# A decoder layer on one core: the feed-forward's input forms made in two steps, row inverses by a product

## The chip, the core and the metric

The kernel runs on one core of a Trainium2 chip. Its engines work in parallel and wait for each other by semaphores: TensorE (PE, matmuls; PEld is its weight load), VectorE (DVE), ScalarE (ACT), GpSimd (POOL), and SyncE (SP, which issues most DMAs). The metric is the device time of one execution, in microseconds.

## What is computed

The layer normalises x, mixes tokens by two kinds of attention, projects the merged mixers and adds the result to the residual. A SwiGLU feed-forward and a last normalisation follow. The part that matters here is the second half:

```python
x = x + merged @ w_out[i]
u2 = rms_norm(x, norm_ffn_g[i])
g_ff, up_ff = jnp.split(u2 @ w_ffn_in[i], 2, axis=-1)
x = x + (jax.nn.silu(g_ff) * up_ff) @ w_ffn_out[i]
return rms_norm(x, norm_final_g)
```

There are 512 tokens, the model is 1024 wide (8 blocks of 128 features) and the feed-forward 2816 wide (22 blocks).

## The kernel before

Everything is kept transposed: features on the 128 partitions, tokens along the free axis. `xall` holds the residual, 8 blocks of 128x512. Each fp32 operand of a matmul is split into a high part (rounded by a copy on ACT) and a low part (the difference, on DVE), and each product is three matmuls: high by high, high by low, low by high (L734, L735, L736, or L157 to L159). Weights come in chunks of 128x1024, split in the same way (L142 on ACT, L143 on DVE); "weights 62" is chunk 62, whose parts the order calls whi62 and wlo62. Three chunks of split weights are held.

**Output projection** (L693 to L702). A loop over f in the order 0, 4, 1, 5, 2, 6, 3, 7 multiplies the merged mixers by one chunk of w_out (24 matmuls of 512 columns), adds the residual into `xall[f]` on DVE (L699), squares it on ACT (L181) and adds the square into `acc2` on POOL (L183). Two PSUM banks alternate. After f = j + 4, `forms(j)` makes what the feed-forward reads of blocks j and j + 4.

**Forms.** The product with w_ffn_in is done by a scheme of 2x2 blocks that needs seven products instead of eight. For it the blocks x[j] and x[j+4], scaled by their gains and cut into two halves of 256 tokens, give B11 and B12 (from x[j]), B21 and B22 (from x[j+4]), and the sums T3 = B22 - B12, U1 = B11 - B12, V2 and T4. The high parts are `fh[j]`, the low parts `fl[j]`, seven pieces of 256 columns each. `forms` runs four multiplies on ACT (L683), splits B11 and B21, makes the four sums on DVE (L685 to L688), and splits the other five pieces together.

**Hidden blocks** (L722). `hidden(i)` runs seven products of 12 matmuls of 256 columns (four j, three matmuls each) in two PSUM banks, `pf` and `pg`. Copies of half-finished sums are kept by ACT (`kept`: q1, q7, wv, yv). It uses four chunks: 62 to 65 for i = 0, 66 to 69 for i = 1, 70 to 73 for i = 2. Because the scale by row comes after the products, block 0 also runs the row statistics: `row_sums` (ss, four sums by matmul from acc2, and r = ms to the power -0.5 on POOL) and `row_spread` (a diagonal matrix dg, one fp32 matmul rb that spreads the row factors over the partitions, and a copy).

**Scaling of the residual.** The feed-forward's rows are not multiplied by the last row factor, so the residual is divided by it instead: after block 1, `scale_residual` takes the reciprocal of the spread row factors on DVE (L715) and multiplies `xall` by it, two blocks at a time (L717). From block 6 on, `down` (the second feed-forward matrix, L808) adds partial products into `xall`.

**Order.** TensorE's instructions follow the order of the code in the feed-forward (`manual_schedule`, L847). On the other engines a scheduler sets the order ahead of time, with `high_priority` for what stands in such a block; on the chip each engine works through its list in order.

Of the kernel before, what the change touches and what calls it, by code (L numbers as in the profile page):

```python
# [10 lines left out]
F32 = mybir.dt.float32  # L11
# [3 lines left out]
ALU = mybir.AluOpType  # L15

P = 128
S = 512
D = 1024
KD = D // P  # L20
# [23 lines left out]
def trunk_kernel(ctx, tc, xT, gains, w_in, w_up, w_o, w_f, w_d, bias, out):  # L44
# [6 lines left out]
    V, A, G, T = nc.vector, nc.scalar, nc.gpsimd, nc.tensor  # L51
# [41 lines left out]
    for step in FFN:  # L93
        if step[0] == "in":
            i = step[1]
            chunks += [("A1", w_f[2 * i], 1024), ("S23", w_f[2 * i + 1], 1024), ("S1", None, 1024), ("S4", None, 512)]
        else:
            _, p, f = step
# [62 lines left out]
    def split_to(hi, lo, src):  # L161
        A.copy(hi, src)  # L162
        V.tensor_tensor(out=lo, in0=src, in1=hi.bitcast(F32), op=ALU.subtract)  # L163
# [15 lines left out]
    def norm_square(k, x, acc, name):  # L179
        sq = acc if k == 0 else sqp.tile([P, S], F32, tag="sq", name=f"sq{name}_{k}")  # L180
        A.activation(sq, x, AF.Square)  # L181
        if k:
            G.tensor_tensor(out=acc, in0=acc, in1=sq, op=ALU.add)  # L183
# [73 lines left out]
    def row_factors(acc, sq, n, name, ps=None, eps=None):  # L257
        if ps is None:
            ps = bank("att", f"ss{name}")
        for t in (acc, sq):  # L260
            for j in range(n if t is not None else 0):
                T.matmul(ps[:, j:j + 1], blk(t, j // 4, j % 4), ones[:, 0:1], start=t is acc and j == 0,
                         stop=t is sq or sq is None, skip_group_check=True)
        ms = cp.tile([P, 8], F32, tag="ms", name=f"ms{name}")
        if eps is None:
            V.tensor_scalar(out=ms[:, :n], in0=ps[:, :n], scalar1=1.0 / D, scalar2=EPS, op0=ALU.mult, op1=ALU.add)
        else:
            V.scalar_tensor_tensor(out=ms[:, :n], in0=ps[:, :n], scalar=1.0 / D, in1=eps, op0=ALU.mult, op1=ALU.add)
        if name == "2":
            rows["eps"] = cp.tile([P, 4], F32, tag="eps", name="eps")  # L270
            V.tensor_scalar_mul(rows["eps"], ms[:, :4], EPS)
        r = cp.tile([P, 8], F32, tag="r", name=f"r{name}")
        G.tensor_tensor(out=r[:, :n], in0=ms[:, :n], in1=mh[:, :n], op=ALU.pow)
        return r
# [63 lines left out]
    def next_weights(ahead=2):  # L338
        w = weights(ci[0], ahead)
        ci[0] += 1  # L340
        return w
# [330 lines left out]
    acc2 = cp.tile([P, S], F32, tag="acc", name="acc2")  # L672
    xall = fp.tile([P, KD, S], F32)
    fh, fl = [], []
    B11, B21, T3, V2, U1, T4, B22 = range(7)

    def forms(j):
        raw = fp.tile([P, 7, hs], F32, tag="form", name=f"form{j}")
        b12 = fp.tile([P, hs], F32, tag="b12", name=f"b12{j}")
        hi = fp.tile([P, 7, hs], F32R, tag=f"fh{j}", name=f"fh{j}")  # L680
        lo = fp.tile([P, 7, hs], F32R, tag=f"fl{j}", name=f"fl{j}")
        for o, k, c in ((raw[:, B11, :], j, 0), (raw[:, B21, :], j + 4, 0), (raw[:, B22, :], j + 4, hs), (b12, j, hs)):
            A.mul(o, xall[:, k, c:c + hs], gt[:, 8 + k:9 + k])  # L683
        split_to(hi[:, 0:2, :], lo[:, 0:2, :], raw[:, 0:2, :])
        V.tensor_tensor(out=raw[:, T3, :], in0=raw[:, B22, :], in1=b12, op=ALU.subtract)  # L685
        V.tensor_tensor(out=raw[:, U1, :], in0=raw[:, B11, :], in1=b12, op=ALU.subtract)
        V.scalar_tensor_tensor(out=raw[:, V2, :], in0=raw[:, B22, :], scalar=-1.0, in1=raw[:, U1, :], op0=ALU.mult, op1=ALU.subtract)
        V.scalar_tensor_tensor(out=raw[:, T4, :], in0=raw[:, V2, :], scalar=-1.0, in1=raw[:, B21, :], op0=ALU.mult, op1=ALU.subtract)  # L688
        split_to(hi[:, 2:, :], lo[:, 2:, :], raw[:, 2:, :])
        fh.append(hi)  # L690
        fl.append(lo)

    for f in HALVES:  # L693
        x = xall[:, f, :]
        nc.gpsimd.dma_start(out=x, in_=xT[f])
        ps = bank("proj", f"po{f}")
        product(ps, mhi, mlo, next_weights(), KD)
        with tc.high_priority():
            V.tensor_tensor(out=x, in0=ps, in1=x, op=ALU.add)  # L699
        norm_square(f, x, acc2, "2")  # L700
        if f >= 4:
            forms(f - 4)  # L702

    def row_sums():
        rows["r2"] = row_factors(acc2, None, 4, "2")
# [4 lines left out]

    def scale_residual():
        inv = sqp.tile([P, S], F32, tag="sq", name="inv")
        V.reciprocal(inv, rows["rb2"])  # L715
        for f in range(0, KD, 2):
            V.tensor_tensor(out=xall[:, f:f + 2, :], in0=xall[:, f:f + 2, :], in1=inv.unsqueeze(1).to_broadcast([P, 2, S]), op=ALU.mult)  # L717


    hh, hl = {}, {}  # L720
# [1 line left out]
    def hidden(i):  # L722
# [15 lines left out]
        def kept(ps, name):  # L738
            t = fp.tile([P, hs], F32, tag=f"kept{name}", name=f"{name}{i}")
            with tc.high_priority():  # L740
                A.copy(t, ps)  # L741
            return t

        w[0] = next_weights()
        if i == 0:

            w[1] = next_weights()
            times(pa, 0, 0, B11, range(3), first=True)
            times(psum, 0, 1, B21, range(3), first=True)
            times(pr, 1, 1, T3, range(3))  # L750
            times(pa, 0, 0, B11, [3])
            q1 = kept(pa, "q1")
            times(psum, 0, 1, B21, [3], last=True)
            times(pr, 1, 1, T3, [3])
            q7 = kept(pr, "q7")
            times(pa, 1, 0, V2)
            wv = kept(pa, "wv")
            with tc.high_priority():
                row_sums()
        else:  # L760
            times(pa, 0, 0, B11, first=True)
            q1 = kept(pa, "q1")
            times(psum, 0, 1, B21, first=True, last=True)
            w[1] = next_weights()
            times(pa, 1, 0, V2)
            wv = kept(pa, "wv")
            times(pr, 1, 1, T3)
            q7 = kept(pr, "q7")
        w[2] = next_weights()
        if i == 0:  # L770
            times(pr, 2, 1, T4, last=True)
# [36 lines left out]
    def down(f, p, w, cs=slice(0, S)):  # L808
        ps = bank("proj", f"pd{p}{f}")[:, cs]
        ks = PARTS[p]  # L810
        product(ps, [hh[k][:, cs] for k in ks], [hl[k][:, cs] for k in ks], w, len(ks))
        x = xall[:, f, cs]
        V.tensor_tensor(out=x, in0=ps, in1=x, op=ALU.add)
        if p < 3:
            return
        if f < KD - 1:
            sq = acc3 if f == 0 else sqp.tile([P, S], F32, tag="sq", name=f"sq3_{f}")
            A.activation(sq[:, cs], x, AF.Square)
            if f:
                G.tensor_tensor(out=acc3[:, cs], in0=acc3[:, cs], in1=sq[:, cs], op=ALU.add)  # L820
        else:
            A.activation(lsq[:, cs], x, AF.Square)
        A.mul(x, x, gt[:, 16 + f:17 + f])
# [25 lines left out]
    for step in FFN:  # L849
        if step[0] == "in":  # L850
            hidden(step[1])
            if step[1] == 1:
                scale_residual()
        elif step[1] < 3 or step[2] < 4:
            down(step[2], step[1], next_weights())
    ws = [next_weights(3 - j) for j in range(4)]
# [92 lines left out]
```

## Time and profile before

| | us |
|---|---|
| median of 3 runs | 782.24 |
| the three runs | 778.64, 782.24, 783.12 |
| the profiled execution | 779.83 |
| its span, first to last instruction | 778.1 |
| TensorE busy | 757.5 |
| DVE busy | 515.6 |
| ACT busy | 363.3 |
| POOL busy | 41.8 |

Matmuls overlap, so the distance from one start to the next tells what one costs, not its own duration. A row of the timeline gives the start, the duration, the engine, the line, the operation and its tiles; in brackets stands how long the engine was idle before it and who released it.

### The profile page before, as it was taken

What the parts mean: (1) busy time and instruction counts of PE and PEld (TensorE: products, weight loads), DVE (VectorE), ACT (ScalarE), POOL (GpSimd) and SP (SyncE); (2) the same over time, 40 slices, a digit from 0 to 9 for tenths busy, and PEclk for the clock granted to TensorE, in tenths of its full rate; (3) what the DMA queues carried; (4) which work ended last, traced back from release to release, by engine and by line L of the source; (5) the groups of instructions that cost most, each with busy time, mean ns of one, the idle gap of its engine ahead of it and who ended that gap; (6) DMA issues with size and microseconds to landing.
All of it is one profiled execution on the core that took longest, in us unless ns stands there. A gap on an engine that the chain in (4) does not pass through costs nothing.

```text
span 778.1 us, 10997 instructions
## 1 busy us (share of the span) xinstructions
PE 757.5 (97%) x4469; PEld 647.7 (83%) x4469; DVE 515.6 (66%) x674; ACT 363.3 (47%) x520; POOL 41.8 (5%) x46
## 2 busy tenths in 40 slices
PE   8999999999999999999997899999999999999994
PEld 5876767788877878888786899999999999999983
DVE  6343636434777773376886999886778777776543
ACT  7273736643223532332664556554445454444362
POOL 1000000000100100002321000000000000000032
PEclk9999999999999999999997999999999999999998
DMA  7421212023222223234521232333333333332113
GB/s 243 136 76 61 81 55 82 28 82 116 74 82 82 73 91 95 64 112 171 183 80 55 81 103 92 111 96 102 96 102 115 103 88 106 113 102 75 43 53 109
DMA packets 24947, 74.13 MB, mean 95 GB/s; under 512 B 2736, under 2 KB 5824, under 8 KB 24768
## 3 DMA queue, kind: packets, MB, share of 16 engines
q1 hardware_dynamic: 23536, 69.74, 28.0%
q0 software_dynamic: 816, 3.16, 1.1%
q8 instruction: 35, 0.57, 0.3%
q10 hardware_dynamic: 544, 0.52, 0.2%
q14 instruction: 16, 0.13, 0.1%
HBM read 71.32 MB, written 2.10 MB: 94 GB/s over the span
## 4 chain that ended last, share of the span: by engine, by line
PE 87%; DVE 7%; ACT 2%; DMA 1%; issue 1%; SPq 0%; POOL 0%; DVEq 0%; ACTq 0%; POOLq 0%
PE pd L157 5%; PE pd L158 5%; PE pd L159 5%; PE pf L736 5%; PE pf L735 5%; PE pf L734 5%; PE pg L734 4%; PE pg L735 4%; PE pg L736 4%; PE pjgs L157 2%; PE pjgd L157 2%; PE pjgs L159 2%; PE pjgd L159 2%; PE pjgs L158 2%; PE pjgd L158 2%; PE pvvd L157 2%
## 5 line engine op out<-in xcount | busy, mean ns | idle before, releaser
L142 ACT CAST whi<-raw 128x1024 fp32r<-128x1024 f32 (+2 forms) x113 | 108.5, 962 | 155.0 <-issue 49.2
L143 DVE TENSOR_TENSOR wlo<-raw,whi 128x1024 fp32r<-128x1024 f32 (+2 forms) x113 | 126.1, 1117 | 36.6 <-ACT whi L142 36.0
L736 PE MATMUL pf<-fh,wlo 128*128 128x256 f32 x352 | 100.4, 285 | 2.1 <-DVE wlo L143 2.1
L734 PE MATMUL pf<-fh,whi 128*128 128x256 f32 x352 | 100.6, 286 | 1.6 <-ACT fh L162 1.0
L735 PE MATMUL pf<-fl,whi 128*128 128x256 f32 x352 | 100.3, 285 | 1.1 <-DVE fl L163 1.1
L734 PE MATMUL pg<-fh,whi 128*128 128x256 f32 x264 | 76.1, 288 | 0.8 <-ACT fh L162 0.8
L735 PE MATMUL pg<-fl,whi 128*128 128x256 f32 x264 | 75.5, 286 | 0.9 <-DVE fl L163 0.9
L736 PE MATMUL pg<-fh,wlo 128*128 128x256 f32 x264 | 75.3, 285 | 0.0
L734 PEld LDWEIGHTS pf<-fh,whi 128*128 128x128 f32 x352 | 68.2, 194 | 3.6 <-ACT yv L741 1.6
L736 PEld LDWEIGHTS pf<-fh,wlo 128*128 128x128 f32 x352 | 68.1, 194 | 2.7 <-DVE wlo L143 2.7
L735 PEld LDWEIGHTS pf<-fl,whi 128*128 128x128 f32 x352 | 68.1, 194 | 1.9 <-DVE fl L163 1.3
L157 PE MATMUL pd<-hh,whi 128*128 128x512 f32 (+1 forms) x184 | 69.3, 377 | 0.0
L158 PE MATMUL pd<-hl,whi 128*128 128x512 f32 (+1 forms) x184 | 69.2, 376 | 0.0
L159 PE MATMUL pd<-hh,wlo 128*128 128x512 f32 (+1 forms) x184 | 69.0, 375 | 0.0
L143 DVE TENSOR_TENSOR wlo<-s,whi 128x1024 fp32r<-128x1024 f32 (+1 forms) x44 | 42.1, 957 | 17.9 <-ACT whi L142 17.9
L734 PEld LDWEIGHTS pg<-fh,whi 128*128 128x128 f32 x264 | 51.3, 194 | 1.5 <-ACT fh L162 1.0
L735 PEld LDWEIGHTS pg<-fl,whi 128*128 128x128 f32 x264 | 51.3, 194 | 1.2 <-DVE fl L163 1.2
L142 ACT CAST whi<-s 128x1024 fp32r<-128x1024 f32 (+1 forms) x44 | 36.8, 837 | 31.1 <-PE pg L735 22.8
L736 PEld LDWEIGHTS pg<-fh,wlo 128*128 128x128 f32 x264 | 51.3, 194 | 0.0
L159 PEld LDWEIGHTS pd<-hh,wlo 128*128 128x128 f32 x184 | 34.6, 188 | 6.4
L157 PEld LDWEIGHTS pd<-hh,whi 128*128 128x128 f32 x184 | 34.7, 189 | 5.9
L158 PEld LDWEIGHTS pd<-hl,whi 128*128 128x128 f32 x184 | 34.7, 189 | 5.7
(437 smaller groups left out, 1660.7 us busy)
## 6 DMA issues: line engine op xcount, KB each, us to landing
raw<-in_w_in_dram SPq DMA_DIRECT2D x44, 512.0 KB, 3.3
rawu<-in_w_ffn_in_dram SPq DMA_DIRECT2D x22, 512.0 KB, 3.2
raw<-in_w_ffn_in_dram SPq DMA_DIRECT2D x22, 512.0 KB, 3.4
raw<-in_w_ffn_out_dram SPq DMA_DIRECT2D x24, 384.0 KB, 3.1
raw<-in_w_out_dram SPq DMA_DIRECT2D x8, 512.0 KB, 3.3
raw<-in_w_up_dram SPq DMA_DIRECT2D x8, 384.0 KB, 3.1
x<-in_xT_dram SPq DMA_DIRECT2D x8, 256.0 KB, 4.4
xall<-in_xT_dram POOLq DMA_DIRECT2D x8, 256.0 KB, 6.4
```

Source lines behind the costliest of these rows:

```text
L142: A.copy(hi, r)
L143: V.tensor_tensor(out=lo, in0=r, in1=hi.bitcast(F32), op=ALU.subtract)
L157: T.matmul(ps, shi, mhi, start=first, stop=False)
L158: T.matmul(ps, shi, mlo, start=False, stop=False)
L159: T.matmul(ps, slo, mhi, start=False, stop=last)
L734: T.matmul(ps, hi[:, cs], xhi, start=first and k == 0, stop=False, skip_group_check=True)
L735: T.matmul(ps, hi[:, cs], xlo, start=False, stop=False, skip_group_check=True)
L736: T.matmul(ps, lo[:, cs], xhi, start=False, stop=last and k == 3, skip_group_check=True)
```

## The change

The forms are made in two steps. `forms_upper(j)` runs right after f = j and makes B11 and U1. `forms_lower(j)` runs right after f = j + 4 and makes B21, B22, T3, V2 and T4: the high parts of B21 and B22 are written by ACT straight from the residual, the others by SCALAR_TENSOR_TENSOR on DVE from the residual, a gain and the piece before. Both stand in a high-priority block, ahead of the square. The forms stand in another order in their tile, and a tile `ng` holds the negated gains. In hidden block 0 all of B11 comes first, and the last quarter (j = 3) of B21, T3 and V2 comes after the other three quarters of all of them. The inverse row factor is the mean square times its power of -0.5; it is spread by a matmul of its own in block 1. The residual is multiplied by it in the first `down` of each block.

```diff
@@ row_factors
-        ms = cp.tile([P, 8], F32, tag="ms", name=f"ms{name}")
+        ms = cp.tile([P, 8], F32, tag="ms", name=f"ms{name}", bufs=2)
...
+            rows["ms2"] = ms
@@ output projection
-    B11, B21, T3, V2, U1, T4, B22 = range(7)
-
-    def forms(j):
-        raw = fp.tile([P, 7, hs], F32, tag="form", name=f"form{j}")
-        b12 = fp.tile([P, hs], F32, tag="b12", name=f"b12{j}")
+    B11, U1, B21, B22, T3, V2, T4 = range(7)
+    ng = cp.tile([P, KD], F32)
+    V.tensor_scalar_mul(ng, gt[:, 8:16], -1.0)
...
+    def forms_upper(j):
+        raw = fp.tile([P, 3, hs], F32, tag="form", name=f"form{j}", bufs=2)
         hi = fp.tile([P, 7, hs], F32R, tag=f"fh{j}", name=f"fh{j}")
         lo = fp.tile([P, 7, hs], F32R, tag=f"fl{j}", name=f"fl{j}")
-        for o, k, c in ((raw[:, B11, :], j, 0), (raw[:, B21, :], j + 4, 0), (raw[:, B22, :], j + 4, hs), (b12, j, hs)):
-            A.mul(o, xall[:, k, c:c + hs], gt[:, 8 + k:9 + k])
-        split_to(hi[:, 0:2, :], lo[:, 0:2, :], raw[:, 0:2, :])
-        V.tensor_tensor(out=raw[:, T3, :], in0=raw[:, B22, :], in1=b12, op=ALU.subtract)
-        V.tensor_tensor(out=raw[:, U1, :], in0=raw[:, B11, :], in1=b12, op=ALU.subtract)
-        V.scalar_tensor_tensor(out=raw[:, V2, :], in0=raw[:, B22, :], scalar=-1.0, in1=raw[:, U1, :], op0=ALU.mult, op1=ALU.subtract)
-        V.scalar_tensor_tensor(out=raw[:, T4, :], in0=raw[:, V2, :], scalar=-1.0, in1=raw[:, B21, :], op0=ALU.mult, op1=ALU.subtract)
-        split_to(hi[:, 2:, :], lo[:, 2:, :], raw[:, 2:, :])
+        A.mul(raw[:, 0:2, :], halves(xall[:, j, :]), gt[:, 8 + j:9 + j])
+        V.tensor_tensor(out=raw[:, 2, :], in0=raw[:, 0, :], in1=raw[:, 1, :], op=ALU.subtract)
+        split_to(hi[:, 0:2, :], lo[:, 0:2, :], raw[:, 0:3:2, :])
...
+    def forms_lower(j):
...
+        A.mul(hi[:, 2:4, :], halves(x), g)
+        V.scalar_tensor_tensor(out=raw[:, 0, :], in0=x[:, hs:], scalar=g, in1=up[:, 1, :], op0=ALU.mult, op1=ALU.subtract)
+        V.scalar_tensor_tensor(out=raw[:, 1, :], in0=x[:, hs:], scalar=n, in1=up[:, 2, :], op0=ALU.mult, op1=ALU.subtract)
+        V.scalar_tensor_tensor(out=raw[:, 2, :], in0=x[:, :hs], scalar=n, in1=raw[:, 1, :], op0=ALU.mult, op1=ALU.subtract)
+        V.scalar_tensor_tensor(out=lo[:, 2:4, :], in0=halves(x), scalar=g, in1=hi[:, 2:4, :].bitcast(F32), op0=ALU.mult, op1=ALU.subtract)
+        split_to(hi[:, 4:, :], lo[:, 4:, :], raw)
...
             V.tensor_tensor(out=x, in0=ps, in1=x, op=ALU.add)
+        with tc.high_priority():
+            if f >= 4:
+                forms_lower(f - 4)
+            else:
+                forms_upper(f)
         norm_square(f, x, acc2, "2")
-        if f >= 4:
-            forms(f - 4)
@@ row factors
-    def scale_residual():
-        inv = sqp.tile([P, S], F32, tag="sq", name="inv")
-        V.reciprocal(inv, rows["rb2"])
-        for f in range(0, KD, 2):
-            V.tensor_tensor(out=xall[:, f:f + 2, :], in0=xall[:, f:f + 2, :], in1=inv.unsqueeze(1).to_broadcast([P, 2, S]), op=ALU.mult)
+    def row_inverse():
+        inv = cp.tile([P, 8], F32, tag="ms", name="msi", bufs=2)
+        V.tensor_tensor(out=inv[:, :4], in0=rows["ms2"][:, :4], in1=rows["r2"][:, :4], op=ALU.mult)
+        rows["inv"] = cp.tile([P, S], F32, tag="acc", name="inv")
+        A.copy(rows["inv"], broadcast_rows(inv, 0, 4, "2i"))
@@ hidden, i == 0
-            times(pa, 0, 0, B11, range(3), first=True)
+            times(pa, 0, 0, B11, first=True)
+            q1 = kept(pa, "q1")
             times(psum, 0, 1, B21, range(3), first=True)
             times(pr, 1, 1, T3, range(3))
-            times(pa, 0, 0, B11, [3])
-            q1 = kept(pa, "q1")
+            times(pa, 1, 0, V2, range(3))
             times(psum, 0, 1, B21, [3], last=True)
             times(pr, 1, 1, T3, [3])
             q7 = kept(pr, "q7")
-            times(pa, 1, 0, V2)
+            times(pa, 1, 0, V2, [3])
@@ hidden, i > 0, after T3
+            if i == 1:
+                with tc.high_priority():
+                    row_inverse()
@@ down
+        if p == 0:
+            V.tensor_tensor(out=x, in0=x, in1=rows["inv"], op=ALU.mult)
         V.tensor_tensor(out=x, in0=ps, in1=x, op=ALU.add)
@@ the loop over the feed-forward's steps
-            if step[1] == 1:
-                scale_residual()
```

Three places of the built order show what moved. The first is TensorE in hidden block 0, where the last pair's forms fh3 and fl3 are read for B21, T3 and V2. Before:

```order
L736 MATMUL pg0_2998<-fh2_2888,wlo63_2943 128x256
L734 MATMUL pf0_2997<-fh3_2979,whi62_2906 128x256
L735 MATMUL pf0_2997<-fl3_2980,whi62_2906 128x256
L736 MATMUL pf0_2997<-fh3_2979,wlo62_2907 128x256
L734 MATMUL pg0_2998<-fh3_2979,whi62_2906 128x256
L735 MATMUL pg0_2998<-fl3_2980,whi62_2906 128x256
L736 MATMUL pg0_2998<-fh3_2979,wlo62_2907 128x256
L734 MATMUL pg0_2998<-fh3_2979,whi63_2942 128x256
L735 MATMUL pg0_2998<-fl3_2980,whi63_2942 128x256
L736 MATMUL pg0_2998<-fh3_2979,wlo63_2943 128x256
L734 MATMUL pf0_2997<-fh0_2712,whi63_2942 128x256
```

The same place now:

```order
L754 MATMUL pf0_2995<-fh2_2848,wlo63_2949 128x256
L752 MATMUL pg0_2996<-fh3_2935,whi62_2905 128x256
L753 MATMUL pg0_2996<-fl3_2936,whi62_2905 128x256
L754 MATMUL pg0_2996<-fh3_2935,wlo62_2906 128x256
L752 MATMUL pg0_2996<-fh3_2935,whi63_2948 128x256
L753 MATMUL pg0_2996<-fl3_2936,whi63_2948 128x256
L754 MATMUL pg0_2996<-fh3_2935,wlo63_2949 128x256
L752 MATMUL pf0_2995<-fh3_2935,whi63_2948 128x256
L753 MATMUL pf0_2995<-fl3_2936,whi63_2948 128x256
L754 MATMUL pf0_2995<-fh3_2935,wlo63_2949 128x256
```

B11's last quarter (pf with whi62) has moved up behind its other three quarters, and three quarters of V2 (pf with fh0 to fh2 and whi63) have moved ahead of all that is shown here.

The second place is DVE around the last residual add (po7) and the last forms; s2367 is a sum of weights for block 1. Before:

```order
L686 TENSOR_TENSOR form3_2977<-form3_2977,b123_2978 128x256
L134 TENSOR_TENSOR s2367_3120<-rawu67_2940,raw66_2904 128x1024
L699 TENSOR_TENSOR xall_2639<-po7_2939,xall_2639 128x512
L143 TENSOR_TENSOR wlo64_3000<-rawu63_2852,whi64_2999 128x1024
L685 TENSOR_TENSOR form3_2977<-form3_2977,b123_2978 128x256
L687 SCALAR_TENSOR_TENSOR form3_2977<-form3_2977 128x256
L163 TENSOR_TENSOR fl3_2980<-form3_2977,fh3_2979 128x512
L688 SCALAR_TENSOR_TENSOR form3_2977<-form3_2977 128x256
L132 TENSOR_TENSOR rawu71_3115<-rawu71_3115 128x512
L163 TENSOR_TENSOR fl3_2980<-form3_2977,fh3_2979 128x1280
```

And now, where forml3 holds T3, V2 and T4:

```order
L690 TENSOR_TENSOR form3_2934<-form3_2934 128x256
L134 TENSOR_TENSOR s2367_3118<-rawu67_2946,raw66_2903 128x1024
L163 TENSOR_TENSOR fl3_2936<-form3_2934,fh3_2935 128x512
L714 TENSOR_TENSOR xall_2639<-po7_2945,xall_2639 128x512
L702 SCALAR_TENSOR_TENSOR forml3_2980<-xall_2639,gt_86,form3_2934 128x256
L703 SCALAR_TENSOR_TENSOR forml3_2980<-xall_2639,ng_2640,form3_2934 128x256
L143 TENSOR_TENSOR wlo64_2998<-rawu63_2859,whi64_2997 128x1024
L705 SCALAR_TENSOR_TENSOR fl3_2936<-xall_2639,gt_86,fh3_2935 128x512
L704 SCALAR_TENSOR_TENSOR forml3_2980<-xall_2639,ng_2640,forml3_2980 128x256
L163 TENSOR_TENSOR fl3_2936<-forml3_2980,fh3_2935 128x768
```

A split of two forms now stands ahead of the add, and the split behind it has three forms instead of five.

The third place is DVE in hidden block 1, at the scaling of the residual. Before:

```order
L715 RECIPROCAL inv_3281<-rb2_3106 128x512
L134 TENSOR_TENSOR s2371_3252<-rawu71_3115,raw70_3074 128x1024
L791 TENSOR_TENSOR g0_3136<-pf0_2997,rb2_3106 128x256
L143 TENSOR_TENSOR wlo68_3152<-rawu67_2940,whi68_3151 128x1024
L143 TENSOR_TENSOR wlo69_3182<-s469_3183,whi69_3181 128x512
L717 TENSOR_TENSOR xall_2639<-xall_2639,inv_3281 128x1024 x4
L143 TENSOR_TENSOR wlo70_3218<-raw70_3074,whi70_3217 128x1024
```

And now:

```order
L143 TENSOR_TENSOR wlo70_3227<-raw70_3072,whi70_3226 128x1024
L835 TENSOR_TENSOR xall_2639<-xall_2639,inv_3215 128x512 x8
L810 SCALAR_TENSOR_TENSOR u1_3278<-q71_3211,yv1_3242 128x256
L808 TENSOR_TENSOR g1_3277<-pg1_3148,q11_3165 128x256
L811 SCALAR_TENSOR_TENSOR u1_3278<-pg1_3148,wv1_3197 128x256
L143 TENSOR_TENSOR wlo71_3259<-s2371_3261,whi71_3258 128x1024
```

The multiplies of the residual now stand in one run behind weights 70, ahead of weights 71, and the reciprocal is gone. TensorE has one more row, the matmul rb2i behind T3 of block 1.

## Rows read from the trace of the kernel before

**Rows 1.** Page: busy us (share) xinstructions; granted clock in 40 slices.

```profile
PE 757.5 (97%) x4469; PEld 647.7 (83%) x4469; DVE 515.6 (66%) x674; ACT 363.3 (47%) x520; POOL 41.8 (5%) x46
PEclk9999999999999999999997999999999999999998
```

**Rows 2.** Stretches: length, busy of PE, PEld, DVE, ACT, POOL, clock, DMA.

```profile
369.50:405.30 35.80, 34.43 (x152) 28.20 (x151) 30.53 (x37) 22.02 (x34) 12.53 (x8) 1.00 0.42 144
...
412.20:422.40 10.20, 8.59 (x39) 8.29 (x40) 5.67 (x11) 3.80 (x8) 1.06 (x1) 0.51 0.15 44
```

**Rows 3.** Timeline of TensorE, hidden block 0: start, duration, operation.

```profile
405.33 0.28 PE L734 MATMUL pf<-fh,whi 128*128 128x256 f32 x1
...
408.44 0.28 PE L736 MATMUL pg<-fh,wlo 128*128 128x256 f32 x1
409.74 0.38 PE L734 MATMUL pf<-fh,whi 128*128 128x256 f32 x1 [1.02 <-ACT fh L162]
411.19 0.38 PE L735 MATMUL pf<-fl,whi 128*128 128x256 f32 x1 [1.06 <-DVE fl L163]
...
412.87 0.58 PE L734 MATMUL pg<-fh,whi 128*128 128x256 f32 x1 [0.83 <-ACT fh L162]
414.40 0.58 PE L735 MATMUL pg<-fl,whi 128*128 128x256 f32 x1 [0.94 <-DVE fl L163]
...
417.34 0.41 PE L736 MATMUL pf<-fh,wlo 128*128 128x256 f32 x1
417.55 1.70 PE L262 MATMUL ss<-ones,acc 128*128 128x1 f32 x8
...
423.47 1.02 PE L286 MATMUL rb<-dg,ones 128*128 128x512 f32 x2
424.92 0.39 PE L734 MATMUL pf<-fh,whi 128*128 128x256 f32 x1 [0.43 <-ACT yv L741]
```

**Rows 4.** Timeline of DVE, the last forms.

```profile
404.40 1.52 DVE L686 TENSOR_TENSOR form<-form,b 128x256 f32<-128x256 f32 x1
...
406.98 0.68 DVE L699 TENSOR_TENSOR xall<-po,xall 128x512 f32<-128x512 f32 x1
...
409.21 0.98 DVE L685 TENSOR_TENSOR form<-form,b 128x256 f32<-128x256 f32 x1 [0.42 <-ACT form L683]
...
412.85 1.49 DVE L163 TENSOR_TENSOR fl<-form,fh 128x1280 fp32r<-128x1280 f32 x1
```

**Rows 5.** Timeline of ACT, the last forms.

```profile
407.75 0.63 ACT L181 ACTIVATE sq<-xall 128x512 f32<-128x512 f32 x1 [1.40 <-DVE xall L699]
408.29 0.89 ACT L683 ACTIVATE form<-xall,gt 128x256 f32<-128x256 f32 x2
...
411.56 1.26 ACT L162 CAST fh<-form 128x1280 fp32r<-128x1280 f32 x1 [1.87 <-DVE form L688]
```

**Rows 6.** Timeline of POOL, the last two sums of squares.

```profile
403.45 2.19 POOL L183 TENSOR_TENSOR acc<-acc,sq 128x512 f32<-128x512 f32 x1 [4.54 <-ACT sq L181]
408.52 1.39 POOL L183 TENSOR_TENSOR acc<-acc,sq 128x512 f32<-128x512 f32 x1 [2.89 <-ACT sq L181]
```

**Rows 7.** Timeline of DVE, the same subtraction for the first pair.

```profile
375.33 0.42 DVE L686 TENSOR_TENSOR form<-form,b 128x256 f32<-128x256 f32 x1
```

**Rows 8.** Timeline of DVE, reciprocal and scaling of the residual.

```profile
426.94 3.35 DVE L715 RECIPROCAL inv<-rb 128x512 f32<-128x512 f32 x1
...
433.34 4.62 DVE L717 TENSOR_TENSOR xall<-xall,inv 128x1024 f32<-128x1024 f32 x4
437.88 1.22 DVE L143 TENSOR_TENSOR wlo<-raw,whi 128x1024 fp32r<-128x1024 f32 x1
```

**Rows 9.** Timeline of TensorE, waits in hidden block 2.

```profile
439.15 0.39 PE L736 MATMUL pf<-fh,wlo 128*128 128x256 f32 x1 [1.36 <-DVE wlo L143]
...
443.09 0.39 PE L736 MATMUL pf<-fh,wlo 128*128 128x256 f32 x1 [0.50 <-DVE wlo L143]
```

**Rows 10.** Timeline of TensorE, four records of a row sum in the tail.

```profile
758.63 0.50 PE L262 MATMUL ss<-ones,acc 128*128 128x1 f32 x4
```

More of the change, by code (lines that the diff above doesn't have):

```diff
@@ L674, in trunk_kernel, with halves @@
     fh, fl = [], []
-    B11, B21, T3, V2, U1, T4, B22 = range(7)
-    def forms(j):
-        raw = fp.tile([P, 7, hs], F32, tag="form", name=f"form{j}")
-        b12 = fp.tile([P, hs], F32, tag="b12", name=f"b12{j}")
+    B11, U1, B21, B22, T3, V2, T4 = range(7)
+    ng = cp.tile([P, KD], F32)
+    V.tensor_scalar_mul(ng, gt[:, 8:16], -1.0)
+    upper = []
+    def halves(t):
+        return t.rearrange("p (a n) -> p a n", a=2)
+    def forms_upper(j):
+        raw = fp.tile([P, 3, hs], F32, tag="form", name=f"form{j}", bufs=2)
@@ L690, in forms @@
+        split_to(hi[:, 0:2, :], lo[:, 0:2, :], raw[:, 0:3:2, :])
+        upper.append(raw)
         fh.append(hi)
         fl.append(lo)
+    def forms_lower(j):
+        k = j + 4
+        x, up, hi, lo = xall[:, k, :], upper[j], fh[j], fl[j]
+        g, n = gt[:, 8 + k:9 + k], ng[:, k:k + 1]
+        raw = fp.tile([P, 3, hs], F32, tag="form2", name=f"forml{j}")
+        A.mul(hi[:, 2:4, :], halves(x), g)
[4 more added lines that the diff above has]
+        split_to(hi[:, 4:, :], lo[:, 4:, :], raw)
```

## The prediction

> **What bounds the kernel now.** The first look goes to the page's busy line [rows 1]: TensorE is busy for 757.5 of 778.1 us, DVE for 515.6 and ACT for 363.3. Only the 20.6 us in which TensorE idles, and whatever it does at a low clock, can be won without taking matmuls out, and the change takes none out. The clock line [rows 1] has one digit under 9 between start and end, in slice 22, which is 408 to 428 us. So the second look is the table of stretches [rows 2]: over 412.2 to 422.4 the granted clock is 0.51, the lower of the two levels (1.2 GHz). In the output projection before it, DVE is busy for 30.53 of 35.80 us, so it has 5.3 us to spare there.
>
> The third look is TensorE's timeline around the start of the feed-forward [rows 3]. The first matmul of hidden block 0 starts at 405.33; 26 matmuls later it is 408.44, so one takes 0.12 us. Then four waits in a row, 1.02, 1.06, 0.83 and 0.94 us, all for the forms of the last pair of residual blocks (fh3, fl3). During the third the clock falls, and a matmul of the same shape now takes 0.21 (417.34 to 417.55). The sums of squares (ss, 8 records) take 1.70 us; in the tail four such records take 0.50 [rows 10], so eight at the full clock need about 0.9.
>
> Why are fh3 and fl3 late? On DVE the last residual add starts only at 406.98 [rows 4], 1.5 us after its product has ended, because a 128x256 subtraction of the form before took 1.52 instead of 0.42 [rows 4, 7]: it stood while POOL's sum of squares ran at 403.45 [rows 6]. Behind the add come ACT's square and two multiplies (407.75, 408.29), a subtraction of 0.98 again beside POOL (409.21), the cast of five forms (411.56, 1.26 us) and their low part (412.85, 1.49 us) [rows 4 to 6]. The chain ends at 414.34, and TensorE's last wait with it.
>
> A second, smaller loss: DVE's reciprocal takes 3.35 us and the four scalings of the residual 4.54 (433.34 to 437.88) [rows 8]. The low part of the weights for hidden block 2 stands behind them, and TensorE waits 1.36 us for it at 439.15 and 0.50 for the next one at 443.09 [rows 9].
>
> **The change, part by part.** All times below are hand replays of the new order with durations from the rows. A DVE instruction is counted start to start: 1.13 us for 1024 columns (4.54 / 4 [rows 8]), 0.60 for 512 and 0.33 for 256 (0.68 and 0.42 less the overlap of some 0.08 [rows 4, 7]).
>
> *Upper forms early.* B11 and U1 of block j need only x[j], so for j = 3 they are made one product (5.4 us) before the feed-forward starts. Their cost is one ACT multiply of 512 columns (0.63 by the square of that width [rows 5]), a subtraction and a split; they lie beside the last product. So the 12 matmuls of B11 find fh3 ready. I put the split's end at about 405.3; it is wanted by the tenth and eleventh matmul, at 406.5.
>
> *TensorE's order.* Block 0 now does all of B11, then three quarters of B21, T3 and V2: 39 matmuls before the first lower form of fh3 is read, instead of 27. That point is 405.33 + 39 x 0.12 = 410.0.
>
> *Lower chain.* The last product ends at 405.5. By the order, DVE has the low part of weights 63, the upper subtraction, a sum of weights and a split ahead of the add; from the end of the product before (about 400.1) that is 0.60 + 1.13 + about 1.6 beside POOL + 1.13 + 0.60, which ends at 405.3. So the add starts at 405.6 and ends at 406.2 (406.98 is the other end, if DVE stays as late as now). Two products of 256 follow (406.9), then the low part of weights 64 (408.0). ACT multiplies B21 and B22 by 406.9 and squares by 407.4. POOL's sum goes in at 408.0 and holds for 1.39 [rows 6]. No row has a SCALAR_TENSOR_TENSOR beside POOL; the nearest are the subtractions, which stood until POOL was through, so I count the low part of B21, B22 as held: 409.4 to 410.0. T4 is done at 410.35, the cast of three forms at 411.2 (between 0.63 for 512 and 1.26 for 1280 columns [rows 5]) and their low part at 412.1. B21's last quarter runs at 410.0 without a wait; T3's last quarter waits 0.8 for the cast and 0.8 for the low part: **1.6 us**. Without the hold it is 0.3; with the add at 406.98 it is 3.0.
>
> The Trainium skill, page "SBUF — State Buffer", section "Who interferes with whom", says that a DVE instruction with two SBUF inputs and a GpSimd instruction that reads SBUF exclude each other for the whole instruction, which covers the four new products as well. By that rule the wait is the 1.6 of the sum, and a kernel whose products were exempt would save 1.3 more; the subtraction of 1.52 us beside POOL agrees with it, and no run here shows a product beside POOL yet.
>
> *The clock.* With one stretch of idling of 1.6 us in place of 3.85 over 6 us I take it that the clock stays up, as it did through the 1.36 at 439.15 (granted clock 1.00 there).
>
> *Inverse row factors.* The reciprocal (3.35 us of DVE) goes. In its place come one tiny DVE product, four 128x128 multiplies shared by DVE and ACT, a copy on ACT, and one more broadcast matmul on TensorE in block 1, which lies fully on the path: 1.02 us, as the two records at 423.47 [rows 3].
>
> *Division.* The diff puts one product in each first `down`; the order shows all eight in one run on DVE behind weights 70, 8 x 0.60 = 4.8 us against 4.54. They stand behind the copy of the inverse on ACT, and behind them stand u and g of block 1 and the low part of weights 71. From the copy of rb2 (417.7) to the end of weights 71 DVE has 16.0 us of work, plus about 1 us of waits for ACT's silu and a transfer: 434.7. TensorE wants it at 434.0 (below). I take a wait of **1.0**; 0 to 2 is possible.
>
> *One product at the start* (the negated gains) is a 128x8 instruction on DVE ahead of work that needs the same gains: nothing on the path.
>
> **The sum.** Block 0 after: 84 x 0.12 = 10.1, ss 0.9, rb 1.0, the wait for yv 0.43 as now [rows 3], T3's wait 1.6, restarts 0.3: 14.3 us. Block 1: 10.1 + 1.0 + 0.15 = 11.25. The third matmul of block 2 then starts at 405.33 + 14.3 + 11.25 + 0.24 = 431.1. Before, it started at 439.15 [rows 9]: 8.0 us gained. The wait for weights 71 is 1.0 instead of 0.50: 0.5 back. **Net 7.5 us.** After block 2 TensorE runs without gaps in both, and the tail is not touched, so it arrives at the end whole. Of the 8.0, about 3.5 are the clock (the 39 records at 0.51 less the 8 of ss are 31 matmuls [rows 2], x 0.09 = 2.8, and 0.7 of ss), 1.36 the wait at 439.15, and the rest shorter waits less 1.0 for the new matmul.
>
> The profiled execution took 779.83 us (span 778.1): by it the changed kernel takes 772.3. It lies 2.4 under the median of the three runs; the mean of all four executions is 781.0, and from that I get 773.5.
>
> **The rivals.**
> 1. *The clock falls all the same.* The two waits of T3 come within 2 us, and before, it fell after two waits of 1.02 and 1.06. Against it: TensorE is busy without a gap up to 410.4, and 1.36 alone did not do it. It costs 3.5 us: 777.0. Chance 0.15.
> 2. *DVE becomes the bound in blocks 1 and 2.* It works in order, and the run of eight cannot start before the inverse is copied. If that is 2 us late, so are weights 71, and TensorE waits 3 us instead of 1: 775.5 to 776. For it: DVE is already busy without a gap from 430 on; against it: it has 3 us less to do. Chance 0.08.
> 3. *Slower: the output projection loses its cover.* Each pair of blocks has about as much DVE work as before (6.9 us against 6.8), but more instructions with two SBUF inputs that can meet one of POOL's eight sums. If each sum holds DVE once more, for 1.4, that is 11.2 us against the 5.3 us to spare [rows 2]: the residual adds come late, TensorE waits for its two banks in every product, some 6 us in all, and two stretches at the low level cost 4.5 us each. That is 15 lost for 7.5 gained: 788. It decides from the point where the projection takes 7.5 us longer. Against it: the holds now seen already include one for nearly every sum. Chance 0.05.
>
> That the division isn't spread, as the diff reads, is visible in the order and is in the sum; spread, it would give 772.5.
>
> **How the numbers follow.** Forecast 0.72, rival 1 0.15, rival 2 0.08, rival 3 0.05. What a measurement can tell from no change is 0.5%, 3.9 us, which puts the bound at 777.1. The forecast and rival 2 are faster; rival 1 lies on the bound and is halved: faster 0.87, same 0.08, slower 0.05. The low end is the forecast without the hold (1.3) and without the wait for weights 71 (1.0), from an execution 1.7 under the mean: 769.5. The high end takes in rival 1 with 0.8 for the spread of the runs: 777.8.
>
> **What would show it.** Right: TensorE's granted clock is 1.00 all over 405 to 430; the first wait in block 0 is in T3's last quarter and lasts under 2 us in all; ss takes 0.9; block 2 starts near 431; no reciprocal; eight products in a run of 4.8 us on DVE; one wait of about 1 us for weights 71. Wrong: a stretch at half clock, waits of TensorE for residual adds before 405, or a start of the feed-forward later than 405.5.

## The result, and the profile after

| | before | after |
|---|---|---|
| median, us | 782.12 | 777.12 |
| lowest and highest | 778.64, 783.48 | 775.46, 780.13 |
| profiled execution, us | 779.83 | 776.87 |
| its span | 778.1 | 775.2 |

The ratio is 0.9945, with a 95% interval of 0.9926 to 0.9963: 0.55% faster, where the forecast's 7.5 us are 1.0% of the 781.0 us it started from. The time lies inside the range and near rival 1 (777.0), 3.6 us above the forecast (773.5).

On the page of the changed kernel, TensorE's busy line and the granted clock in 40 slices, which answer to [rows 1]:

```profile
PE 756.3 (98%) x4471; PEld 646.6 (83%) x4471; DVE 515.1 (66%) x685; ACT 360.9 (47%) x515; POOL 42.6 (5%) x46
PEclk9999999999999999999999999999999999999998
```

The digit under 9 in the middle has gone from the clock line, but a digit is a mean over 19 us. Stretches show more; the columns are those of [rows 2]. The first is the output projection from 369.5 on, the next two lie in hidden block 0:

```profile
369.50:407.00 37.50, 35.73 (x158) 29.28 (x157) 32.26 (x41) 20.00 (x28) 11.55 (x10) 1.00 0.44 153
407.07:417.90 10.83, 7.89 (x59) 7.08 (x58) 9.90 (x13) 5.26 (x10) 3.59 (x2) 1.00 0.13 48
417.90:421.30 3.40, 3.40 (x18) 3.40 (x17) 2.48 (x8) 1.46 (x6) 2.11 (x1) 0.50 0.31 76
```

For 3.40 us TensorE still runs at the lower level. TensorE's timeline of block 0, which answers to [rows 3]:

```profile
407.07 0.28 PE L752 MATMUL pf<-fh,whi 128*128 128x256 f32 x1
...
408.14 0.28 PE L752 MATMUL pf<-fh,whi 128*128 128x256 f32 x1
409.49 0.39 PE L753 MATMUL pf<-fl,whi 128*128 128x256 f32 x1 [1.07 <-DVE fl L163]
409.71 0.28 PE L754 MATMUL pf<-fh,wlo 128*128 128x256 f32 x1
...
413.85 0.39 PE L753 MATMUL pg<-fl,whi 128*128 128x256 f32 x1 [0.51 <-DVE fl L705]
...
415.11 0.38 PE L752 MATMUL pg<-fh,whi 128*128 128x256 f32 x1 [0.76 <-ACT fh L162]
416.10 0.39 PE L753 MATMUL pg<-fl,whi 128*128 128x256 f32 x1 [0.61 <-DVE fl L163]
...
416.80 0.94 PE L262 MATMUL ss<-ones,acc 128*128 128x1 f32 x8
...
418.15 0.41 PE L752 MATMUL pg<-fh,whi 128*128 128x256 f32 x1
418.36 0.41 PE L753 MATMUL pg<-fl,whi 128*128 128x256 f32 x1
...
422.05 1.02 PE L287 MATMUL rb<-dg,ones 128*128 128x512 f32 x2
423.50 0.39 PE L752 MATMUL pf<-fh,whi 128*128 128x256 f32 x1 [0.43 <-ACT yv L759]
```

Four waits again, 1.07, 0.51, 0.76 and 0.61 us. The first is for the upper split of fl3, which was to be ready before the block began. Then the clock falls, and a matmul takes 0.21 us (418.15 to 418.36) instead of 0.12.

DVE and POOL around the last two residual adds, which answer to [rows 4, 6]:

```profile
400.51 1.78 DVE L705 SCALAR_TENSOR_TENSOR fl<-xall,gt,fh 128x512 fp32r<-128x512 f32 x1
...
404.46 0.68 DVE L714 TENSOR_TENSOR xall<-po,xall 128x512 f32<-128x512 f32 x1
...
407.66 1.77 DVE L163 TENSOR_TENSOR fl<-form,fh 128x512 fp32r<-128x512 f32 x1
409.36 0.68 DVE L714 TENSOR_TENSOR xall<-po,xall 128x512 f32<-128x512 f32 x1
...
412.01 1.78 DVE L705 SCALAR_TENSOR_TENSOR fl<-xall,gt,fh 128x512 fp32r<-128x512 f32 x1
```

```profile
399.96 1.78 POOL L183 TENSOR_TENSOR acc<-acc,sq 128x512 f32<-128x512 f32 x1 [2.57 <-ACT sq L181]
406.57 2.31 POOL L183 TENSOR_TENSOR acc<-acc,sq 128x512 f32<-128x512 f32 x1 [4.83 <-ACT sq L181]
411.46 1.78 POOL L183 TENSOR_TENSOR acc<-acc,sq 128x512 f32<-128x512 f32 x1 [2.58 <-ACT sq L181]
```

Each low part of 512 columns ends 0.55 us after a sum of POOL's: 407.66 + 1.77 = 409.43 against 406.57 + 2.31 = 408.88, and 413.79 against 413.24, as if it had begun only when the sum was nearly through. The last product ends at 407.2 and its add starts at 409.36, so the add is 2.1 us late. Before it was 1.5 late [rows 4] in the first profile and 2.2 in a second one, so this lateness is no new loss.

Block 2, on DVE, ACT and TensorE, in place of [rows 8, 9]:

```profile
433.33 4.90 DVE L835 TENSOR_TENSOR xall<-xall,inv 128x512 f32<-128x512 f32 x8
...
438.48 0.41 DVE L808 TENSOR_TENSOR g<-pg,q 128x256 f32<-128x256 f32 x1
...
439.15 1.21 DVE L143 TENSOR_TENSOR wlo<-s,whi 128x1024 fp32r<-128x1024 f32 x1
```

```profile
438.92 0.62 ACT L142 CAST whi<-s 128x512 fp32r<-128x512 f32 x1 [1.83 <-DVE g L808]
439.44 0.36 ACT L759 COPY q<-pf 128x256 f32<-128x256 f32 x1
```

```profile
439.86 0.39 PE L752 MATMUL pf<-fh,whi 128*128 128x256 f32 x1 [0.86 <-ACT q L759]
...
440.41 0.39 PE L754 MATMUL pf<-fh,wlo 128*128 128x256 f32 x1
```

TensorE waits 0.86 us for ACT's copy of q of block 2. The run of eight products keeps g of block 1, and g frees the buffer into which q is copied; but the copy starts 0.55 us after g has ended, right behind a cast of weights that stands ahead of it in ACT's list. That cast starts at 438.92. Here its wait is put down to g, which ends at 438.89. In six other profiles with this division the same wait of 1.83 us is put down to TensorE's second product of the block, whose last matmul with the high part of the weights ends at 438.88 here. So the times don't tell which of the two the cast waited for, and g alone does not explain the whole wait. The low part of weights 71 ends at 440.36 (439.15 + 1.21), and the matmul that reads it starts at 440.41: it is late as well, behind the wait for q.

By blocks (first matmul of a block to the first of the next), from the two profiles: block 0 took 21.12 before and 17.96 after, block 1 10.95 and 10.93, block 2 12.94 and 11.65. That is 4.5 us. Block 0 starts 1.74 us later after (407.07 against 405.33), so the spans differ by 2.9. Of the 1.74, 1.35 us stand ahead of the output projection, whose first matmul starts at 361.49 against 360.14: there the profile after has a stretch of 3.4 us at the low level, from 32.2 on, that the one before has not, and both kernels have the same instructions. The rest is one wait early in the projection, behind the load of x (1.77 us at 374.30 against 1.37 at 372.55). So the later start, which the prediction had named as a sign of being wrong, does not come from the change.

### The profile page after: what moved, and what is told of

Read it like the earlier page. It is cut to its first block, busy times and chain, and to the rows that moved or that the text cites. A ratio compares the mean times of both kernels' runs of the same rounds, so it can differ in the third digit from the quotient of the medians.

```text
span 775.2 us, 10995 instructions
## 1 busy us (share of the span) xinstructions
PE 756.3 (98%) x4471; PEld 646.6 (83%) x4471; DVE 515.1 (66%) x685; ACT 360.9 (47%) x515; POOL 42.6 (5%) x46
```

## The experiments

The theory: DVE's list is short enough, but POOL's sums hold it, so the forms are late, TensorE's waits add up, and the clock falls. The rivals: the list itself is too long; TensorE's new order gives nothing; the low clock is not a matter of these waits.

**POOL's sums cut to 8 columns**, in the changed kernel and in the kernel before. The kernels leave out the other 504 columns of each sum; DVE, ACT and TensorE keep their lists.

```diff
-            G.tensor_tensor(out=acc, in0=acc, in1=sq, op=ALU.add)
+            G.tensor_tensor(out=acc[:, :8], in0=acc[:, :8], in1=sq[:, :8], op=ALU.add)
```

> The changed kernel, but POOL adds only the first 8 of 512 columns of each square into the sum, so POOL hardly runs while the forms are made (the sums of squares are then wrong for the other columns). All lists of DVE and ACT are the same. Theory 1 (DVE is held by POOL's sums, and that made the lower chain late): no form instruction on DVE lasts longer than alone (0.42 for 256 columns, about 0.7 for 512); the last residual add starts within 0.5 us of the end of its product instead of 2.0; block 0, from its first matmul to the first of block 1, falls from 18.0 to about 14.3 us, and the clock stays up; 3 to 4 us less than the changed kernel. Rival (the list itself is too long: a weight split, a weight sum and a form split stand ahead of the add): the add still starts 1.5 us or more after the product, block 0 stays at 16.5 or more, and 1 us or less is gained.

Measured: 772.52 us, ratio to before 0.9898 (0.9869 to 0.9927). DVE's and TensorE's timeline of this kernel:

```profile
405.31 0.68 DVE L163 TENSOR_TENSOR fl<-form,fh 128x512 fp32r<-128x512 f32 x1
407.26 0.69 DVE L714 TENSOR_TENSOR xall<-po,xall 128x512 f32<-128x512 f32 x1 [1.27 <-PE po L159]
...
409.93 0.75 DVE L705 SCALAR_TENSOR_TENSOR fl<-xall,gt,fh 128x512 fp32r<-128x512 f32 x1
```

```profile
412.98 0.39 PE L753 MATMUL pg<-fl,whi 128*128 128x256 f32 x1 [0.61 <-DVE fl L163]
```

With the same list DVE now stands idle 1.27 us for the last product, and the add starts as soon as it ends (407.26 against 407.23); the add of the product before comes 0.2 us behind its product, where it had come 2.7. One wait for forms is left, the clock stays up through block 0, and the block takes 14.06 us. The list is not too long; the sums hold it.

> The kernel before with the same cut: POOL adds only the first 8 columns of each square (sums wrong for the others). Theory 1: the four waits for the last forms shrink too, since the subtractions of 1.52 and 0.98 us fall back to 0.42: about 1.1 + 0.6 us less wait, block 0 from 21.0 to 18 to 19 if the clock still falls, about 16 if it stays up. Rival: block 0 stays above 20.

Measured: 779.33 us, ratio 0.9981 (0.9967 to 0.9994), block 0 17.85 us. DVE's and TensorE's timeline of this one:

```profile
414.20 0.69 DVE L132 TENSOR_TENSOR rawu<-rawu 128x512 f32<-128x512 f32 x1 [1.40 <-DMA rawu<-in_w_ffn_in_dram]
414.81 1.48 DVE L163 TENSOR_TENSOR fl<-form,fh 128x1280 fp32r<-128x1280 f32 x1
```

```profile
416.35 0.58 PE L735 MATMUL pg<-fl,whi 128*128 128x256 f32 x1 [1.76 <-DVE fl L163]
```

Without the holds the old forms come earlier too: their low part ends 7.6 us after the block's start (416.29 against 408.65), where it had been 9.0 in the first profile of before. It would be ready 0.7 us sooner still, but it stands behind a step of the weights that waits for a transfer. Block 0 comes out just under the 18 to 19 us of the theory, with a stretch of 3.4 us at the low level. The same cut is worth 0.2% in the kernel before and, by the two ratios, 0.5% in the changed one.

**Each half of the change alone**: the new forms with the old reciprocal and scaling, then the inverse and the division alone with the old forms.

> The forms in two steps and the new order of matmuls in block 0, with the division as before (reciprocal and four scalings after block 1). Both theories: block 0 as in the changed kernel, 18.0 us. The waits for weights 70 and 71 return in block 2 (1.9 us against 0.9 in the changed kernel), but the broadcast matmul of block 1 (0.85) is gone: 0 to 1 us slower than the changed kernel, 3 to 4 us faster than before, ratio about 0.995.

Measured: 778.61 us, ratio 0.9972 (0.9957 to 0.9987). Block 0 took 17.76 us, as in the whole change, block 2 12.88, as before. The median is 1.5 us above the changed kernel's, where 0 to 1 was expected.

> The division alone (inverse by a product, spread by a matmul, one product per down in the code), with the forms and the order of block 0 as before. Both theories: block 0 stays at 21.0 us with the low clock; blocks 1 and 2 together gain 0.5 to 1.5 us; ratio 0.998 to 0.9995, so hardly to be told from no change.

Measured: 780.45 us, ratio 0.9990 (0.9975 to 1.0004). Block 2 took 11.62 us with the same wait of 0.86 for q, as in the whole change. Block 0 took 19.30, not 21.0: its waits are about as long as before (3.5 us), but the stretch at the low level lasts 3.4 us. Each half does in its own block what it does in the whole. The gains of 0.28% and 0.10% add up to less than the 0.55% of both, a difference inside the intervals, and the second alone can't be told from no change.

**The sums on DVE**, the same computation. The last sum falls into a gap in which DVE waits for ACT's cast of three forms.

```diff
-            G.tensor_tensor(out=acc, in0=acc, in1=sq, op=ALU.add)
+            V.tensor_tensor(out=acc, in0=acc, in1=sq, op=ALU.add)
```

> The changed kernel with the seven sums of squares of the residual moved from POOL to DVE, same computation. Theory 1 (DVE is held by POOL's sums, the amount of DVE work is not the trouble): a sum costs DVE 0.6 us instead of holding it 1.1 to 1.4; the last two sums fall into gaps in which DVE waits for ACT's casts. The last residual add starts within 0.3 us of its product's end, waits for forms under 1 us in all, block 0 takes 14.0 to 14.6 us with no half-clock stretch in it, and the time is 772.5 to 773.5 us. Rival (4.2 us more DVE work makes the chain late all the same): last add 0.5 us or more late, block 0 over 16 us, 775 us or more.

Measured: 773.82 us, ratio 0.9896 (0.9874 to 0.9919). DVE's timeline:

```profile
408.62 0.69 DVE L714 TENSOR_TENSOR xall<-po,xall 128x512 f32<-128x512 f32 x1 [0.68 <-PE po L159]
...
411.28 0.75 DVE L705 SCALAR_TENSOR_TENSOR fl<-xall,gt,fh 128x512 fp32r<-128x512 f32 x1
411.94 0.48 DVE L704 SCALAR_TENSOR_TENSOR forml<-xall,ng,forml 128x256 f32<-128x256 f32 x1
412.34 0.69 DVE L183 TENSOR_TENSOR acc<-acc,sq 128x512 f32<-128x512 f32 x1
```

The add again waits for its product, block 0 takes 14.07 us at the full clock, and the median is 0.3 us above the range of the expectation. Doing the sum (0.6 us from start to start) is cheaper for DVE than standing beside it (1.03 for L705: 1.78 less 0.75).

**POOL's sums in four pieces of 128 columns**, with the lists of the others as they are.

```diff
-            G.tensor_tensor(out=acc, in0=acc, in1=sq, op=ALU.add)
+            for c in range(0, S, P):
+                G.tensor_tensor(out=acc[:, c:c + P], in0=acc[:, c:c + P], in1=sq[:, c:c + P], op=ALU.add)
```

> The changed kernel with each of POOL's seven sums of 512 columns cut into four of 128; the lists of DVE, ACT and TensorE are the same. A sum of 512 takes 1.29 us alone and one of 256 0.73, so a piece should take about 0.45 and a sum 1.8 in all. If the hold is for one POOL instruction and DVE gets in between two of them: the low part of 512 columns beside a sum takes at most 1.2 us instead of 1.78, the last residual add starts within 0.6 us of its product's end, block 0 takes 14.5 to 16 us, 773 to 775 us. If POOL's next piece goes first each time: the low part takes 1.8 us or more, block 0 17.5 to 18.5 us, 777 us or more.

Measured: 773.41 us, ratio 0.9893 (0.9874 to 0.9911), block 0 14.46 us. DVE's and POOL's timeline:

```profile
406.07 0.95 DVE L163 TENSOR_TENSOR fl<-form,fh 128x512 fp32r<-128x512 f32 x1
...
410.25 0.95 DVE L706 SCALAR_TENSOR_TENSOR fl<-xall,gt,fh 128x512 fp32r<-128x512 f32 x1
```

```profile
409.70 2.84 POOL L184 TENSOR_TENSOR acc<-acc,sq 128x128 f32<-128x128 f32 x4 [1.53 <-ACT sq L181]
```

The sum becomes longer (2.84 us, where the whole one took 1.78), and yet the low part beside it shrinks from 1.78 to 0.95. So the hold lasts for one instruction of POOL's, and DVE gets in between two of them.

**The division spread**: each product is held back until the hidden block before its `down` has been split.

```diff
-        split_to(hi, lo, g)
+        rows["split"] = split_to(hi, lo, g)
...
-            V.tensor_tensor(out=x, in0=x, in1=rows["inv"], op=ALU.mult)
+            d = V.tensor_tensor(out=x, in0=x, in1=rows["inv"], op=ALU.mult)
+            tc.add_manual_dep(d.ins, rows["split"].ins.name, NOSYNC, reason="issue order")
```

> The changed kernel with each of the eight products of residual and inverse held back in the order until the hidden block before its first down product is split, same computation. Theory (the run of eight on DVE, 4.9 us, keeps g and u of block 1 and so ACT's copy of q in block 2): the wait of 0.86 us in block 2 goes, block 2 takes 10.7 to 11.0 us instead of 11.65, 776.2 to 776.5 us. Rival A (DVE is full in blocks 1 and 2 anyway, the wait only moves to the low part of the weights): block 2 over 11.4 us, 777 us. Rival B (each product now delays the first add of its down product and a bank of it): waits of 0.3 us or more at the first down products, 777 to 779 us.

Measured: 775.11 us, ratio 0.9921 (0.9900 to 0.9942). The median is 1.1 us under the range expected. Block 2 took 10.23 us, not the 10.7 to 11.0 expected: TensorE has no wait left in it, and none from there to 640 us; the products now stand between 490 and 566. DVE's timeline in block 1 and ACT's in block 2:

```profile
433.02 0.43 DVE L808 TENSOR_TENSOR g<-pg,q 128x256 f32<-128x256 f32 x1 [0.55 <-PE pg L754]
```

```profile
435.90 0.38 ACT L759 COPY q<-pf 128x256 f32<-128x256 f32 x1 [0.51 <-PE pf L754]
```

g now waits 0.55 us for TensorE and starts 1.2 us before block 2 does (434.26), where it had started 2.5 us after (438.48 against 435.96). The low part of weights 71 is early too (ready at 435.3). And ACT's list has changed with it: the copy of q now stands ahead of the cast of weights (437.27), which it had followed. So this kernel shows that the run of eight products cost the wait, but not whether by g, by the place of the cast in ACT's list or by the low part of the weights. Neither rival is seen.

**Both together**, the sums on DVE and the division spread.

> The changed kernel with the sums of squares on DVE and the division spread. If the two losses are independent: block 0 14.0 to 14.6 us, block 2 10.7 to 11.0 us, 771.6 to 772.7 us, 0.8 below the kernel with the sums alone. If the division's wait only moves: as the kernel with the sums alone.

Measured: 771.77 us, ratio 0.9868 (0.9841 to 0.9895), block 0 14.04 us and block 2 10.23. Both blocks are as short as in the kernel that has each repair alone, so the two losses are independent. The gain over the sums alone is 2.1 us, more than the 0.8 expected. This median is the lowest of all; the interval still overlaps that of the sums alone.

**TensorE's old order of block 0** in the changed kernel.

> The changed kernel with TensorE's old order in block 0 (three quarters of B11, B21 and T3, then their last quarters, then all of V2). Theory (the order is worth the nine matmuls of V2 it puts ahead of the late forms): with forms as late as in the changed kernel TensorE idles 3 us in a row for fl3 of B21, and V2 runs 1.1 us later: block 0 19.1 to 20.5 us by the clock, 778.2 to 779.5 us. Rival (the end of the lower forms alone sets the end of block 0, the order gives nothing): block 0 17.9 to 18.3 us, 777 us.

Measured: 780.21 us, ratio 0.9982 (0.9967 to 0.9997), block 0 21.73 us. TensorE's timeline:

```profile
413.48 0.39 PE L753 MATMUL pg<-fl,whi 128*128 128x256 f32 x1 [2.58 <-DVE fl L705]
...
415.31 0.58 PE L752 MATMUL pg<-fh,whi 128*128 128x256 f32 x1 [1.32 <-ACT fh L162]
416.30 0.58 PE L753 MATMUL pg<-fl,whi 128*128 128x256 f32 x1 [0.41 <-DVE fl L163]
```

The old order idles 2.58 us in a row, and the stretch at the low level that follows lasts 10.24 us, as in the first profile of before. Undoing the order takes back 3.1 us (780.21 - 777.12), most of the gain. Block and time lie above what was expected, by 1.2 and 0.7 us at the upper ends.

**A second profile of each kernel, unchanged.**

> The kernel before, unchanged, for a second profile of block 0. If the stretch of 10.24 us at the low clock in the first profile was one of several outcomes: 3.4 us of it here and block 0 at 19.0 to 19.6 us. If it belongs to the program: 10.24 us again and 21.1 us.

Measured: 778.98 us in one execution; block 0 took 20.02, between the two outcomes that were named. A stretch of it:

```profile
412.20:419.00 6.80, 5.61 (x25) 5.02 (x25) 3.60 (x5) 2.99 (x5) 0.00 (x0) 0.51 0.01 4
```

> The changed kernel, unchanged, for a second profile of block 0. The waits of DVE, ACT and TensorE in block 0 are the same to 0.1 us (they follow from the lists); the stretch at the low clock is there again, for 3.4 us, or is absent if it hangs on less than the waits: then block 0 takes 16.4 us.

Measured: 779.76 us in one execution; block 0 took 18.19. Two stretches of it and TensorE's waits:

```profile
409.24:417.30 8.06, 6.22 (x47) 5.62 (x46) 7.13 (x9) 3.88 (x6) 2.25 (x2) 0.99 0.19 65
417.30:424.10 6.80, 6.80 (x34) 6.80 (x34) 4.40 (x13) 2.97 (x7) 1.97 (x1) 0.50 0.24 77
```

```profile
414.66 0.39 PE L753 MATMUL pg<-fl,whi 128*128 128x256 f32 x1 [0.47 <-DVE fl L705]
...
415.92 0.38 PE L752 MATMUL pg<-fh,whi 128*128 128x256 f32 x1 [0.76 <-ACT fh L162]
416.91 0.39 PE L753 MATMUL pg<-fl,whi 128*128 128x256 f32 x1 [0.61 <-DVE fl L163]
```

The three lower waits repeat to 0.04 us. The first one (1.07, for the upper split) is not there: TensorE had lost time earlier in the projection (a wait of 1.84 us at 374.81 and a stretch of 3.4 us at the low level behind it), the block started at 409.24, and the split was ready. That part of the expectation fell, and the 3.4 us for the stretch with it. The clock fell for 6.80 us: 24 matmuls at 0.21 instead of 0.12 and 0.8 more for ss, some 3.0 us. Block 0 without that would be 15.2.

Block 0 by the stretch at the low level in it, over all profiles: 10.24 us in the first of before and in the one with the old order; 6.8 us in the second of before and the second of after; 3.4 us in the first of after and with each half of the change alone, with the division spread and with the sums cut in the kernel before; none in the four changed kernels in which POOL's sums are cut short, in pieces or on DVE (14.04 to 14.46 us).

## Why the prediction was wrong

The median lies 3.6 us above the forecast, and block 0 alone makes as much: 14.3 us were summed, 17.96 and 18.19 measured in the two profiles. Of the difference the clock makes 1.5 and 3.0 us, the wait for the upper split 1.1 and 0, the longer waits for the lower forms 0.3 and 0.2, and restarts 0.7 and 0.5. A wait costs about 0.26 us beyond its idle time: from 408.14 to 409.49 pass 1.35 us for 1.07 of idle and a matmul of 0.12, and the matmul behind takes 0.22. For the waits of block 0 that is 1.0 and 0.8, where 0.3 was counted.

*The clock* is the step that failed. The prediction took the granted clock to stay up through one stretch of idling of 1.6 us. The second profile of after has nearly that stretch (0.47 + 0.76 + 0.61 = 1.84 us, no other wait in the block before it), and the clock fell behind it. That is rival 1, priced at 3.5 us with 777.0; the two profiles give 1.5 (16 matmuls, 0.21 for 0.12) and 3.0, and the median is 777.12. The rival was given 0.15, because the 1.36 us of [rows 9] had not brought the clock down. One wait was set against three within 2.7 us: the row was too far from the case. Where one wait of 0.6 us for forms is left, the clock stays up, in four kernels. That the median meets rival 1's time is in part luck: rival 1 is the clock alone, and the profiles have other losses beside it.

*Lower chain.* The hold was foreseen and its size was right: L705 took 1.78 us beside POOL and 0.75 without, 1.03 where 1.3 was counted, and T3's waits were 1.88 and 1.84 (B21's share included) where 1.6 was. The start was wrong: the add came 2.1 us behind its product's end in the first profile and 0.8 in the second, not 0.1. That T3's waits came out near the forecast in the first profile all the same is luck, since TensorE itself had been held 1.07 us by then.

*Upper forms early.* This is the second term that was mis-sized. The replay let DVE begin with the add of the product before when that product ended (400.1 in its times). In the first profile this add starts at 404.46, 2.7 us behind its product: DVE was still at the lower forms of the pair before, whose low part had been held by a sum too (1.78 us, beside the sum at 399.96). From that add to the last one the replay had 5.5 us (its terms add to 405.2, not 405.3) and the trace has 4.9. There the hold was foreseen, but on the subtraction (1.6 counted, 0.42 taken); it fell on the split (1.77). The split ended at 409.4, 2.4 us after the start of the block and not with it, and TensorE waited 1.07 us in one of two profiles.

The Trainium skill, page "SBUF — State Buffer", section "Who interferes with whom", says that a DVE instruction with two SBUF inputs and a GpSimd one that reads SBUF exclude each other; the prediction put it beside the upper subtraction and L705. The trace agrees with it for the last three low parts of 512 columns that met a sum (1.77 to 1.78 against 0.68 to 0.75 us), and POOL's sums beside them take longer too (1.78 to 2.31; the shortest in the second profile of after took 1.29).

*TensorE's order* was right in kind and worth more than its 12 matmuls: undone, it costs 3.1 us. Without it the three waits for the lower forms add up to 4.31 us instead of 1.88, and the stretch at the low level is 10.24 us.

*Inverse row factors.* The new matmul costs 0.85 us in block 1 (431.76 - 430.79 less one matmul of 0.12) where 1.02 was counted, but the block is not longer (10.93 against 10.95): waits for weights there, 0.27 and 0.09 us in the first profile of before and 0.62 in the second, each with its restart, went. The forecast had 0.3 more for the block.

*Division.* One wait of about 1 us came, 0.86, but for the copy of q, which the prediction had not followed through ACT's list. Its own reason was there as well: the low part of weights 71 was ready at 440.36, and without the wait for q TensorE would have wanted it at about 439.1 (an estimate: the second product's last matmul starts at 438.72, and three of 0.12 follow), some 1.3 us earlier. So the mechanism was right, and the wait for q covers it. Spread, the division gave 2.0 us (1.4 by the rows of block 2), where 1.0 was forecast.

*The base.* Block 0 of the profile of before (21.12 us) was a long draw: the second profile has 20.02 for the same list, and the same forms with the new division 19.30. A gain read from that one profile was some 1 us too large.

*One product at the start* had no price that can be seen. Rivals 2 and 3 are not seen (rival 3 counted eight sums where there are seven, and its 4.5 us for a stretch at the low level was worked out from no row). In the output projection TensorE is busy for 95% of the stretch shown, against 96% before [rows 2], so POOL's holds cost it next to nothing there, though they make the last add late.

The breakdown of the 8.0 us does not close: its named parts (3.5 for the clock, 1.36, 2.25 for shorter waits, less 1.0) make 6.1, and the restarts of the old waits are in what is left.

What stays open is what brings the clock down and what sets the length of a stretch at the low level. The same list gave 10.24 and 6.8 us before, 3.4 and 6.8 after. And all thirteen profiles have one wait of TensorE early in the output projection, behind the load of x, with no other wait near it. Behind waits of 1.84, 1.89 and 1.99 us (the second profile of after, both repairs together, the division alone) a stretch of 3.4 us at the low level followed; behind eight of 1.35 to 1.83 us, and behind 2.02 and 2.38, none did. So a single wait can do it too, and its length alone does not decide.

## What to carry to other kernels

When work is moved earlier on DVE, replay POOL's instructions beside it as well, each one that the moved work can meet, and count a hold for every two-input step. If POOL's work is short, give it to DVE or cut it into pieces: here that was worth nearly as much as the change itself (0.5% and 0.55%). Begin the replay where DVE really stands, not where a product ends. Where several short waits stand close together in front of TensorE, price the fall of its clock as the likely case, and take the length of a block from two profiles before a gain is read from it.

## What was not expected of the hardware

A sum of 512 columns cut into four took POOL 2.84 us instead of 1.78 and still freed DVE, whose low part fell from 1.78 to 0.95 us. And the stretches at the low level in block 0 came in three lengths, 3.4, 6.8 and 10.24 us; one and the same list gave two of them, before and after.
